# Up projection in three products: all rounded-weight products of a block ahead of all remainder products

## The chip, the core and the metric

The kernel runs on one core of one Trainium2 chip. The metric is the device time of one execution in microseconds (us), less is better. The engines are named as in the profile: PE is TensorE's matmul stream and PEld its weight loads, DVE is VectorE, ACT is ScalarE, POOL is GpSimd, SP is SyncE, whose queue issues the DMAs here.

## What is computed

The reference is a decoder trunk of two layers on 256 tokens of width 1024. Each layer has an attention part and then a feed-forward part, which is where the change lies:

```python
h = _rms_norm(x, g_pre_mlp[l])
y = jnp.square(jax.nn.relu(h @ w_up[l])) @ w_down[l]     # w_up 1024 x 4096, w_down 4096 x 1024
x = x + _rms_norm(y, g_post_mlp[l])
```

All of it is float32.

## The kernel before

**Three products for one.** Most large matmuls are done in the type fp32r on operands split in two: `hi`, the operand rounded to fp32r by ACT (a Copy), and `lo`, what the rounding left over, made by DVE (raw minus hi). A product a x w is taken as a_hi w_hi + a_hi w_lo + a_lo w_hi, all three summed in one PSUM bank. For the weights these tiles are `whi` and `wlo`, made from `wraw`, into which a DMA on SP's queue loads 512 KB (`Weights.load` and `Weights.get`, lines 418 to 446). There are 4 raw slots and 7 slots each of `whi` and `wlo` (lines 43, 421, 440, 441).

**The up projection** (`up`, lines 1319 to 1344). The 4096 columns of w_up are worked off in 8 chunks of 512. Chunk 0 has a form of its own (`up0`). Chunks 1 to 7 call `up(fc)`, and each has four blocks b of 128 columns: 2 layers x 7 chunks x 4 = 56 blocks. A block multiplies 128 columns of weights (the stationary operand, loaded into the array by an LDWEIGHTS for each matmul) with the normalized activations, transposed, in `xT`. `xT[0]` is their rounded half, `xT[1]` the remainder, and `xT[2]` is both side by side: 2 x 256 columns. For each of the 8 slices k of 128 rows there are two matmuls into one PSUM bank `ps` (tag `s`, three of them) of 512 columns:

- the wide one (line 1326): `hi[:, k]` against `xT[2][:, k]`, 512 columns. It puts w_hi x_hi into the left half of the bank and w_hi x_lo into the right half;
- the narrow one (line 1328): `lo[:, k]` against `xT[0][:, k]`, 256 columns, which adds w_lo x_hi into the right half, `ps[:, S:]`.

Behind the block, ACT copies the right half to `h` and DVE adds the left half to it (lines 1335, 1336). Behind every second block ACT and DVE make relu, square and the split of the result into `aT` (lines 1337 to 1343), the operand of the down projection. In the profile, the wide product is `s<-xT,whi`, the narrow one `s<-xT,wlo`.

**The loop around it** (lines 1385 to 1425). `up(fc + 1)` is recorded ahead of the down projection of chunk fc, so that the results of a chunk are needed only one chunk later. The down projection has, for each of 4 slices k, 2 token tiles and 2 column halves, three wide products (512 columns, `mm3`, line 598) into the banks `x` and `acc`: 12 for a k, 48 for a chunk. `then` (line 1330) is the late half of `up0`: four transposes of `h2` and their split.

**What sets the order.** Nothing runs in the order of the source by itself. `Recorder.add` (line 189) notes each operation with its dependences, and `Recorder.order` (line 243) plays a model of the engines: whenever an engine is free, it takes among the operations whose inputs are ready the one with the lowest key (the key is the place in the recording, or that of an earlier mark for loads and splits, lines 429 and 439), urgent ones first. `emit` (line 343) then issues all instructions from one line, 350, in that order. So every row of the profile bears L350, and groups are told apart by tiles.

**A narrow run elsewhere.** In the input projection, `in_chunk_T` (line 1005) has 128 columns of weights as stationary operand against 256 columns of `xT` with `mm3`, three matmuls in a row into the same half of a bank `acc`: `acc<-xT,whi` and `acc<-xT,wlo` in the profile.

Of the kernel before, what the change touches and what calls it, by code (L numbers as in the profile page):

```python
# [460 lines left out]
def trunk(nc, A, consts_in, out, sbp, pp):  # L461
    def tile(shape, dtype, name, tag=None, bufs=1):
        return nc.tile(sbp[(tag or name) not in OPERANDS], shape, dtype, name, tag, bufs)

    def psum(tag):
        return nc.tile(pp, [P, 512], F32, tag, tag, {"acc": 2, "x": 2, "s": 3, "o": 1}[tag], psum=True)

    def small(shape, name, bufs=2):
        return tile(shape, F32, name=name, tag=name, bufs=bufs)
# [49 lines left out]
    def weight(*key):  # L519
        return W.get(index[key])  # L520
# [209 lines left out]
    for l in range(DEPTH):  # L730
# [588 lines left out]
        def up(fc, then=None):  # L1319
            a = [tile([P, 4, S], F32R, name="aT", tag=f"act{j}", bufs=2) for j in range(2)]  # L1320
            for b in range(4):
                hi, lo = weight(l, "up", fc, b)

                ps = psum("s")
                for k in range(8):
                    nc.tensor.matmul(ps, hi[:, k, :], xT[2][:, k].rearrange("p j n -> p (j n)"), start=k == 0, stop=False,
                                     skip_group_check=True)
                    nc.tensor.matmul(ps[:, S:], lo[:, k, :], xT[0][:, k, :], start=False, stop=k == 7,
                                     skip_group_check=True)
                if then is not None and b == 1:  # L1330
                    then()
                if b % 2 == 0:
                    h = tokt("h")
                d = h[:, (b % 2) * S:(b % 2) * S + S]
                nc.scalar.activation(d, ps[:, S:], AF.Copy)
                nc.vector.tensor_add(d, ps[:, :S], d)
                if b % 2:
                    rl = small([P, 512], "rl")
                    nc.scalar.activation(rl, h, AF.Relu)
                    nc.vector.tensor_mul(h, rl, rl)  # L1340
                    d = [y[:, b - 1:b + 1, :].rearrange("p b n -> p (b n)") for y in a]
                    nc.scalar.activation(d[0], rl, AF.Square)
                    nc.vector.tensor_sub(d[1], h, d[0].bitcast(F32))
            return a
# [42 lines left out]
        for fc in range(8):  # L1387
            if fc < 7:
                nxt = up(fc + 1, then)
                then = None  # L1390
# [75 lines left out]
```

## Time and profile before

| | |
|---|---|
| device time, median of 3 runs | 635.33 us (635.32 to 635.46) |
| device time of the profiled execution | 635.77 us |
| its span | 634.0 us |
| mean granted clock of TensorE | 0.998 |
| busy in the span: PE, PEld, DVE, ACT | 625.5, 520.4, 480.9, 373.8 us |
| moved by DMA | 115.75 MB, 183 GB/s over the span |

The span goes from the first to the last recorded instruction; the device time has 1.77 us more around it. In the rows of a group stand: line, engine, operation, output tile <- input tiles, partitions x elements and type, count, then busy us, the mean of one in ns, and the idle time of the engine ahead of them with what ended it. A timeline row has start and duration in us first; "x2" says that two were merged, and the duration is then that of both. Matmuls overlap, and their ends are modelled, so the distance between two starts is what one costs. A row of the chain in order of time has start, duration and the engine with its output tile; "x64" says that it merges 64 instructions. A row of the waits has the us in total, how many times, and the longest. Some matmul records are missing from a trace, so counts from the program go ahead of counts of rows.

### The profile page before, as it was taken

Reading aid. Unit: us, or ns where it says so; the run is one execution under the profiler, and the core shown is the slowest. Engines: PE = TensorE matmul, PEld = TensorE weight load, DVE = VectorE, ACT = ScalarE, POOL = GpSimd, SP = SyncE. Lnnn points to the kernel's source line nnn. Section 1 sums busy time; section 2 is a strip of 40 time slices with the busy share of each in tenths; the row PEclk is TensorE's granted clock in tenths of the full one; section 3 lists DMA queues with packets and bytes.
Section 4 is the critical chain, followed back from the end, with each engine's and each line's share of the span. In section 5 each row is a group of like instructions: output and inputs, shape, how many; then the busy total and the mean of one; then the engine's idle time right before and its main releaser. Section 6 shows DMA issues by size and latency. Waiting matters only on the chain.

```text
span 634.0 us, 9913 instructions
## 1 busy us (share of the span) xinstructions
PE 625.5 (99%) x3570; PEld 520.4 (82%) x3570; DVE 480.9 (76%) x1084; ACT 373.8 (59%) x737; POOL 0.2 (0%) x4
## 2 busy tenths in 40 slices
PE   9999999999999999999999999999999999999995
PEld 6888977688888888888888988777888888888884
DVE  6899998869985665566598999987998665666544
ACT  7865676564864455456467656864658464455432
POOL 0000000000000000000000000000000000000000
PEclk9999999999999999999999999999999999999999
DMA  8998436225786666656329954432267766655601
GB/s 307 345 321 284 131 100 168 85 67 174 247 280 196 196 178 197 194 185 183 121 81 308 331 167 130 166 101 67 66 230 259 228 184 197 197 184 186 197 1 66
DMA packets 47005, 115.75 MB, mean 183 GB/s; under 512 B 4003, under 2 KB 14573, under 8 KB 46957
## 3 DMA queue, kind: packets, MB, share of 16 engines
q1 hardware_dynamic: 46956, 115.13, 56.8%
q8 instruction: 28, 0.46, 0.3%
q14 instruction: 21, 0.16, 0.1%
HBM read 114.07 MB, written 1.05 MB: 182 GB/s over the span
## 4 chain that ended last, share of the span: by engine, by line
PE 98%; DMA 1%; DVE 0%; ACT 0%; SPq 0%; issue 0%; DVEq 0%
PE s L350 35%; PE acc L350 31%; PE x L350 25%; PE o L350 7%; DMA wraw<-in_w_in_dram 1%; SPq L350 0%; DVE x L350 0%; DVE m L350 0%; DVEq L1462 0%; ACT whi L350 0%; ACT xT L350 0%; DVE rsqrt L350 0%; ACT rl L350 0%; DVEq L350 0%
## 5 line engine op out<-in xcount | busy, mean ns | idle before, releaser
L350 DVE TENSOR_TENSOR wlo<-wraw,whi 128x1024 fp32r<-128x1024 f32 (+2 forms) x196 | 230.2, 1180 | 101.8 <-ACT whi L350 100.1
L350 ACT ACTIVATE whi<-wraw 128x1024 fp32r<-128x1024 f32 (+2 forms) x196 | 199.7, 1025 | 157.0 <-PE acc L350 74.2
L350 PE MATMUL s<-xT,whi 128*128 128x512 f32 x448 | 158.5, 397 | 0.0
L350 PE MATMUL s<-xT,wlo 128*128 128x256 f32 x448 | 125.7, 281 | 0.0
L350 PEld LDWEIGHTS s<-xT,whi 128*128 128x128 f32 x448 | 84.1, 188 | 20.5
L350 PE MATMUL acc<-whi,aT 128*128 128x512 f32 x256 | 88.9, 391 | 0.0
L350 PE MATMUL x<-whi,aT 128*128 128x512 f32 x256 | 88.8, 391 | 0.0
L350 PEld LDWEIGHTS s<-xT,wlo 128*128 128x128 f32 x448 | 84.6, 189 | 0.6
L350 PEld LDWEIGHTS x<-whi,aT 128*128 128x128 f32 x256 | 47.9, 188 | 10.2
L350 PEld LDWEIGHTS acc<-whi,aT 128*128 128x128 f32 x256 | 48.0, 188 | 10.0
L350 ACT ACTIVATE pr<-pr,st 128x128 f32<-128x128 f32 (+1 forms) x96 | 42.8, 447 | 17.5 <-DVE st L350 17.1
L350 PE MATMUL acc<-wlo,aT 128*128 128x512 f32 x128 | 49.9, 390 | 0.0
L350 PE MATMUL x<-wlo,aT 128*128 128x512 f32 x128 | 49.9, 390 | 0.0
L350 PE MATMUL acc<-xT,whi 128*128 128x256 f32 x256 | 49.4, 285 | 0.0
L350 PEld LDWEIGHTS acc<-xT,whi 128*128 128x128 f32 x256 | 40.4, 190 | 2.3 <-issue 1.4
L350 PE MATMUL x<-whi,xT 128*128 128x512 f32 x112 | 37.9, 408 | 0.5 <-ACT whi L350 0.3
L350 PE MATMUL acc<-whi,xT 128*128 128x512 f32 (+1 forms) x128 | 38.2, 359 | 0.0
L350 PE MATMUL acc<-xT,wlo 128*128 128x256 f32 x128 | 36.3, 286 | 0.0
L350 ACT ACTIVATE rl<-x 128x512 f32<-128x512 f32 x24 | 14.7, 612 | 24.9 <-PE x L350 16.8
L350 PEld LDWEIGHTS acc<-wlo,aT 128*128 128x128 f32 x128 | 24.0, 188 | 5.1
L350 PEld LDWEIGHTS x<-wlo,aT 128*128 128x128 f32 x128 | 24.0, 188 | 4.6
L350 ACT ACTIVATE h<-s 128x256 f32<-128x256 f32 x56 | 20.6, 368 | 10.7 <-PE s L350 10.7
(219 smaller groups left out, 963.2 us busy)
## 6 DMA issues: line engine op xcount, KB each, us to landing
wraw<-in_w_up_dram SPq DMA_DIRECT2D x64, 512.0 KB, 3.7
wraw<-in_w_down_dram SPq DMA_DIRECT2D x64, 512.0 KB, 3.9
wraw<-in_w_in_dram SPq DMA_DIRECT2D x39, 512.0 KB, 5.0
wraw<-in_w_out_dram SPq DMA_DIRECT2D x16, 512.0 KB, 3.6
w<-in_cmp_w_k_dram SPq DMA_DIRECT2D x8, 512.0 KB, 5.4
w<-in_cmp_w_v_dram SPq DMA_DIRECT2D x8, 512.0 KB, 8.2
wraw<-in_w_in_dram SPq DMA_DIRECT2D x8, 288.0 KB, 5.1
x<-in_x_dram SPq DMA_DIRECT2D x4, 256.0 KB, 7.4
```

The source lines that it names most:

```text
L350: getattr(getattr(self.nc, op.engine), name)(*[real(v) for v in args], **{k: real(v) for k, v in kw.items()})
```

## The change

In `up`, the loop over k is cut in two. In each block the eight wide products of `hi` are recorded first, then the eight narrow ones of `lo`, where before they alternated. The first product still starts the sum in the bank (`start=k == 0`), and the last narrow one still ends it (`stop=k == 7`). No instruction is added or taken away.

```diff
@@ -1325,6 +1325,7 @@
                 for k in range(8):
                     nc.tensor.matmul(ps, hi[:, k, :], xT[2][:, k].rearrange("p j n -> p (j n)"), start=k == 0, stop=False,
                                      skip_group_check=True)
+                for k in range(8):
                     nc.tensor.matmul(ps[:, S:], lo[:, k, :], xT[0][:, k, :], start=False, stop=k == 7,
                                      skip_group_check=True)
                 if then is not None and b == 1:
```

## The prediction

> **What bounds the kernel now.** I read the page's busy line first, then its chain that ended last, to see which engine sets the end.
>
> ```profile
> span 634.0 us, 9913 instructions
> ## 1 busy us (share of the span) xinstructions
> PE 625.5 (99%) x3570; PEld 520.4 (82%) x3570; DVE 480.9 (76%) x1084; ACT 373.8 (59%) x737; POOL 0.2 (0%) x4
> ...
> PE 98%; DMA 1%; DVE 0%; ACT 0%; SPq 0%; issue 0%; DVEq 0%
> ```
>
> TensorE is busy for 99% of the span and is 98% of the chain. A busy TensorE can still hide waits, so the third view is the waits of PE alone:
>
> ```profile
> PE o L350 <- DVE warm L350: 1.2, 1, 1.2
> PE x L350 <- ACT whi L350: 0.3, 1, 0.3
> PE x L350 <- ACT xT L350: 0.2, 1, 0.2
> ```
>
> These 1.7 us are all it shows, and none is in the up projection. So what counts is the distance between the starts of successive matmuls ("pitch"), and the change can act only on that, or by making a new wait. The fourth view is the groups, for the instructions that the change moves.
>
> ```profile
> L350 PE MATMUL s<-xT,whi 128*128 128x512 f32 x448 | 158.5, 397 | 0.0
> L350 PE MATMUL s<-xT,wlo 128*128 128x256 f32 x448 | 125.7, 281 | 0.0
> ...
> L350 PEld LDWEIGHTS s<-xT,whi 128*128 128x128 f32 x448 | 84.1, 188 | 20.5
> ...
> L350 PEld LDWEIGHTS s<-xT,wlo 128*128 128x128 f32 x448 | 84.6, 189 | 0.6
> ```
>
> 448 wide products (512 columns, rounded weights) and 448 narrow ones (256 columns, remainders): 56 blocks of 8 pairs. Their means, 397 and 281 ns, overlap with the next matmul, so they are no prices. Prices come from the fifth view, the chain in order of time, where a piece is so many matmuls in so many us:
>
> ```profile
> 464.32 8.09 PE s L350 x47
> ...
> 482.88 11.29 PE s L350 x64
> 494.17 1.40 PE x L350 x6
> 495.57 1.38 PE acc L350 x6
> 496.95 1.36 PE x L350 x6
> 498.31 1.36 PE acc L350 x6
> ```
>
> The reader is to see three things. Four blocks of the up projection (64 matmuls) take 11.29 us, so 2.822 us a block and 352.8 ns a pair. The down projection behind them, all wide, runs its later passes at 1.36 / 6 = 226.7 ns, but its first twelve at 1.40 + 1.38. And the first chunk of each layer, same instructions, is quicker: 47 matmuls (24 narrow, 23 wide) in 8.09 us; 23 wide ones at 226.7 take 5.21, which leaves 2.88 / 24 = 120 ns for a narrow one, or 346.7 a pair. So there are two paces, 6 ns a pair apart, and I do not know what switches them. The timeline of PE gives the twelve more exactly:
>
> ```profile
> 494.00 0.40 PE L350 MATMUL x<-whi,aT 128*128 128x512 f32 x1
> ...
> 496.79 0.39 PE L350 MATMUL x<-whi,aT 128*128 128x512 f32 x1
> ```
>
> 2.79 / 12 = 232.5 ns for a wide product at the slow pace.
>
> **What a narrow product costs in a run.** The up projection never runs two narrow ones in a row. The input projection does (256 columns, 128x128 weights from the same kind of tile, every matmul with its own weight load, three in a row into the same half bank):
>
> ```profile
> 66.10 0.39 PE L350 MATMUL acc<-xT,whi 128*128 128x256 f32 x2
> ...
> 68.83 0.29 PE L350 MATMUL acc<-xT,wlo 128*128 128x256 f32 x1
> ```
>
> 23 matmuls start from the first to the last of these: 2.73 / 23 = 118.7 ns. With the 120 above, the narrow product has the bounds 118.7 and 120; I take 118.7, as it is the row with narrow neighbours.
>
> **The change, part by part.**
>
> *Removed and added:* nothing. 8 wide and 8 narrow products, with their 16 loads, stay in each block. Only the order of the 16 changes. The planner takes the ready instruction that was recorded first, and both orders are recorded in the loop, so the new order reaches the chip.
>
> *The pitch in the 50 slow blocks* (48 of the later chunks, and the first block of each layer): before, 2.822 us. After, 8 x 232.5 + 8 x 118.7 = 2.810 us, when a run of eight wide products keeps the pace that wide products show right behind the up projection today. That is -0.012 us a block, -0.6 us in all. With 120 ns for the narrow ones it is 2.820 us, and -0.1 us in all. With 226.7 ns for the wide ones it is 2.763 us, -0.059 a block. I take 232.5: the only place where wide products follow narrow ones now is the head of the down projection, and there the slow pace lasts for twelve of them, more than the eight of a run.
>
> *The 6 fast blocks* (three in each layer) take 8.09 + 0.23 us for three, 2.77 each. If they come to the same 2.81, they lose 0.04 each: +0.2 us.
>
> *The wait for the remainders.* In the second block of each layer PE had to go to other work, as the remainder was not there:
>
> ```profile
> 152.25 0.40 PE L350 MATMUL s<-xT,whi 128*128 128x512 f32 x1
> 152.49 0.60 PE L350 MATMUL s<-cst,h 128*128 128x128 f32 x4
> 152.85 0.71 PE L350 MATMUL x<-whi,aT 128*128 128x512 f32 x2
> 153.40 0.28 PE L350 MATMUL s<-xT,wlo 128*128 128x256 f32 x1
> ```
>
> Two wide products take 0.55 us here against 0.45 at 226.7: 0.10 us is lost. After, eight wide products stand between the first use of the rounded weights and that of the remainders, 1.86 us. -0.1 us in each of two layers, -0.2 us. What is late next is nothing that I can see: the transposes of h then wait for the end of their block instead of filling this hole.
>
> *Buffers and the other engines.* The last reader of the rounded weights is now the eighth instruction of a block, not the fifteenth; that of the remainders stays the last. ACT and DVE around one block's end:
>
> ```profile
> 507.84 1.06 ACT L350 ACTIVATE whi<-wraw 128x1024 fp32r<-128x1024 f32 x1 [1.63 <-PE s L350]
> 508.81 0.37 ACT L350 ACTIVATE h<-s 128x256 f32<-128x256 f32 x1
> ...
> 508.93 1.23 DVE L350 TENSOR_TENSOR wlo<-wraw,whi 128x1024 fp32r<-128x1024 f32 x1 [1.47 <-ACT whi L350]
> 510.07 0.42 DVE L350 TENSOR_TENSOR h<-s,h 128x256 f32<-128x256 f32 x1
> ```
>
> ACT's rounding waits for PE to free a slot. It will start about 7 x 118.7 = 0.8 us earlier, DVE's remainder follows ACT and then waits for the last narrow product itself, and the load on SP's queue that reuses the raw slot goes out up to 0.8 us earlier. Queued behind ACT's wait is only the evacuation h, which needs the block's end anyway. No DMA is added, none passes another. All this has seven weight slots and three PSUM banks of slack and is hidden by the PE stream: price 0. If that cover were gone, a block could lose the 1.23 us of one remainder; the waits of PE show no such case even now, with everything 0.8 us later. The evacuation reads both halves of the bank and still comes behind the sixteenth product.
>
> **Sum:** -0.6 + 0.2 - 0.2 = -0.6 us. The profiled execution took 635.77 us, 1.77 beside its span of 634.0; the median of the runs shown, 635.33, is 0.44 lower, and I apply the difference to it: 634.7 us.
>
> **A rule that speaks against it.** The loads: 188 ns each by the groups above, longer than a narrow pitch. Today each load that has only a narrow product as cover stands next to one that has a wide product. In a run of eight, seven loads follow each other with narrow cover only. The Trainium skill, "TensorE: Matmul & The Clock Gate", section "LDWEIGHTS (loading the stationary operand)", gives columns / 1.2 GHz, an estimate of 107 ns for 128 columns, and its section "Back-to-back issue gap" says that the spacing in a real stream is set by both the load and the matmul. By that page 256 columns stream in an estimated 109 ns, so that a run of narrow products would be left with 2 ns of slack a load, and the order of the products would be free only while nothing delays a load. The trace agrees in part: the narrow run goes at 118.7 ns with a load for each.
>
> **The rivals.**
>
> 1. *Faster: the alternation itself holds the slow pace.* If the change of width at each step causes the 6 ns, the runs go at 226.7 + 118.7: 50 x -0.059 = -3.0 us; the head of the down projection loses its excess too, 1.40 + 1.38 - 2 x 1.36 = 0.06 us in each of 12 chunks, -0.7; with the -0.2 of the wait, 631.4 us. For it: the later passes of the down projection, uniform, are fast. Against it: alternating blocks are fast too in the first chunk (8.09 us), and the twelve uniform products are slow. A mixture, in which a run loses the excess midway, gives about 633.
>
> 2. *Slower: weight loads bound the narrow runs.* Place: products 10 to 16 of each block. Price: other narrow stretches are worse than the one above, such as
>
> ```profile
> 62.79 0.36 PE L350 MATMUL acc<-xT,wlo 128*128 128x256 f32 x1
> ...
> 65.63 0.63 PE L350 MATMUL x<-kx,qS 128*128 128x512 f32 x2
> ```
>
> 23 matmuls in 2.84 us, 123.5 ns. That is 4.8 ns more on 448 products, +2.2 us on the forecast: 636.9 us. It decides (0.2% = 1.3 us above before; 0.2% is about what a measurement of this kernel can tell from no change) from 4.2 ns a narrow product above 118.7, (1.3 + 0.6) / 448. The far bound, loads not hidden at all at 188 ns, would be +31 us. Against it: this stretch holds its excess in its first start after transposes; behind that it keeps 120 ns.
>
> 3. *The change does nothing on the chip:* the planner could give back the alternation, where remainders are ready. Its keys follow the recording, so I give this no chance of its own; it would be 635.3.
>
> **How the numbers follow.** Forecast (order nearly neutral, 634.4 to 635.6): 0.42. Rival 1 with its mixture: 0.34. Rival 2, with any other reshuffling by the planner that makes PE wait: 0.24. The range reaches half into each rival: 632.0 to 637.0 us. Faster by over 0.2%: 0.34; within: 0.42; slower: 0.24.
>
> **What would show it.** In the chain, four blocks should be one piece of 64 matmuls in 11.24 us (11.05 by rival 1, 11.4 or more by rival 2). In the timeline, eight wide starts 232 ns apart and eight narrow ones 119 apart; rival 2 shows in the narrow ones alone. The first twelve of the down projection should keep their 2.78 us, and rival 1 takes them to 2.72. The hole at 152.85 should be gone, and PE's waits should be no more than the three lines above. ACT's rounding should start in mid-block. What would make me wrong: the two paces, whose cause I do not know; a pace that spreads from the runs into the 36 later products of each down chunk would cost more than all terms here.

## The result and the profile after

The changed kernel takes 633.49 us (median of 7 runs, 633.02 to 633.63), the kernel before 635.46 us beside it (7 runs, 635.02 to 635.94). The ratio is 0.9967, 95% interval 0.9955 to 0.9979: 0.33% faster, 2.0 us. That is inside the range, but not the case forecast as likeliest (nearly neutral, 634.7 us); it lies where rival 1 put its mixture, at about 633. The forecast gain was 0.6 us, less than a third of the one measured.

First the page of the changed kernel, the lines that answer to those shown of before:

```profile
span 631.8 us, 9913 instructions
PE 622.8 (99%) x3570; PEld 520.6 (82%) x3570; DVE 482.1 (76%) x1084; ACT 373.6 (59%) x737; POOL 0.2 (0%) x4
...
PE 96%; DMA 2%; DVE 1%; ACT 1%; issue 0%; SPq 0%; DVEq 0%
```

As many instructions as before, the same engine at the end, a span that is 2.2 us shorter. The waits of PE are the same three as before:

```profile
PE o L350 <- DVE warm L350: 1.2, 1, 1.2
PE x L350 <- ACT whi L350: 0.7, 1, 0.7
PE x L350 <- ACT xT L350: 0.2, 1, 0.2
```

The middle one is longer (0.7 us, 0.3 before), but it falls at 7.7 us, long ahead of the first up projection, and in a second profile of the changed kernel (e_after, below) it is 1.4: it is no part of the change. Now its chain in order of time (start, duration, engine and output tile, instructions merged):

```profile
459.26 11.59 PE s L350 x68
...
481.75 11.15 PE s L350 x64
492.90 1.39 PE x L350 x6
494.28 1.36 PE acc L350 x6
```

Four blocks went from 11.29 to 11.15 us; this piece stands in 12 chunks, so -1.7 us. The head of the down projection behind them, its first twelve products, went from 1.40 + 1.38 to 1.39 + 1.36: -0.03 us, -0.4 in the 12. The first chunk of a layer is one piece of 68 now (64 products and the four transposes), 11.59 us. The chain of the kernel before has it in three pieces, of which the last is the 8.09 us of the prediction:

```profile
460.36 3.49 PE s L350 x21
463.85 0.47 PE x L350 x2
```

That is 12.05 us together, with two down products in it, which cost 0.45 elsewhere. So nothing was won there. -1.7 and -0.4 give -2.1 us: the measured 2.0 lies in the up projection and the twelve products behind it.

Where inside the 11.15? The timeline of PE. In a merged row the duration ends with the last instruction, so the distance to the next row's start is what a run costs:

```profile
481.59 1.98 PE L350 MATMUL s<-xT,whi 128*128 128x512 f32 x8
483.40 1.11 PE L350 MATMUL s<-xT,wlo 128*128 128x256 f32 x8
484.35 2.00 PE L350 MATMUL s<-xT,whi 128*128 128x512 f32 x8
486.19 1.12 PE L350 MATMUL s<-xT,wlo 128*128 128x256 f32 x8
487.15 2.00 PE L350 MATMUL s<-xT,whi 128*128 128x512 f32 x8
```

The first wide run of a chunk, behind the down projection's wide products, takes 483.40 - 481.59 = 1.81 us, 226 ns each. The later ones, behind a narrow run, take 1.84 (230 ns each). The narrow runs take 0.95 to 0.96, 119 ns each. So a wide run behind a narrow one is 0.03 us longer than its pure price, and so is the head of the down projection. If each product at the slow pace costs 232.5 - 226.7 = 5.8 ns too much, 30 ns are five of them, not eight and not twelve. The trace, which holds the starts to the nanosecond, shows these five: from 484.35 us on, the eight distances are 234, 235, 229, 232, 231, then 227, 226, 227 ns.

### The profile page after: what moved, and what is told of

Its sections match the earlier page's. It is cut to its first block, busy times and chain, and to the rows that moved or that the text cites. A ratio compares the mean times of both kernels' runs of the same rounds, so it can differ in the third digit from the quotient of the medians.

```text
span 631.8 us, 9913 instructions
## 1 busy us (share of the span) xinstructions
PE 622.8 (99%) x3570; PEld 520.6 (82%) x3570; DVE 482.1 (76%) x1084; ACT 373.6 (59%) x737; POOL 0.2 (0%) x4
## 4 chain that ended last, share of the span: by engine, by line
PE 96%; DMA 2%; DVE 1%; ACT 1%; issue 0%; SPq 0%; DVEq 0%
PE s L350 35%; PE acc L350 30%; PE x L350 24%; PE o L350 7%; DMA wraw<-in_w_in_dram 1%; DMA xt<-in_xT_dram 1%; DVE q L350 0%; ACT whi L350 0%; ACT xT L350 0%; ACT q_tok L350 0%; DVE rope L350 0%; SPq L350 0%; DVE x L350 0%; DVE m L350 0%; DVEq L1463 0%
## 5 line engine op out<-in xcount | busy, mean ns | idle before, releaser
L350 PE MATMUL s<-xT,whi 128*128 128x512 f32 x448 | 112.0, 392 | 0.0
L350 PEld LDWEIGHTS s<-xT,whi 128*128 128x128 f32 x448 | 81.4, 189 | 15.2
L350 PEld LDWEIGHTS s<-xT,wlo 128*128 128x128 f32 x448 | 61.1, 190 | 4.4
L350 PE MATMUL s<-xT,wlo 128*128 128x256 f32 x448 | 62.5, 282 | 0.0
```

The source lines that it names most:

```text
L350: getattr(getattr(self.nc, op.engine), name)(*[real(v) for v in args], **{k: real(v) for k, v in kw.items()})
```

## The experiments

The question is what makes wide products slow. Three theories. *Changes:* each step from narrow to wide costs something, so what counts is how many such steps a chunk has. *Counts:* each narrow product leaves a debt that the wide ones behind it pay, so the order is nearly free. *Release:* the gain comes from the weight slots that come free earlier, not from PE. The pure price of four blocks is 32 x 226.7 + 32 x 119.4 = 11.07 us. The diffs below are shortened, and words in brackets stand for code. Those of e_fours, e_late, e_wide and e_quad are written against the changed kernel, the others against the kernel before; only e_fours, e_late and e_wide show removed lines. All times stand beside the kernel before on the same chip: 635.73 us in the first and the last group, 635.51 and 635.54 in the others.

### Two blocks at a time (e_pairs)

```diff
+                if b % 2 == 0:
+                    two = []
+                    for i in range(2):
+                        two.append((*weight(l, "up", fc, b + i), psum("s")))
+                    for hi, lo, ps in two:
+                        for k in range(8):
+                            (wide product)
+                    for hi, lo, ps in two:
+                        for k in range(8):
+                            (narrow product)
+                ps = two[b % 2][2]
```

> Two blocks at a time: 16 wide products, then 16 narrow ones. Without any slow pace four blocks would take 11.07 us (32 x 226.7 + 32 x 119.4 ns). The changed kernel shows 11.15, that is 28 ns for each of its three changes from narrow to wide inside a chunk, and 2.75 instead of 2.72 us for the first twelve products of the down projection. Theory of changes (a fixed 28 ns for each change from narrow to wide): one change inside a chunk instead of three, 11.10 us, head of the down projection 2.75; 14 chunks x 0.056 = 0.8 us less than the changed kernel, 632.7 us. Theory of counts (3.5 ns for each narrow product, repaid by the wide ones behind it): 56 ns behind each run of 16, 11.13 us, head 2.78, no gain, 633.5 us. Theory of release (the gain comes from the weight slot that comes free earlier): the slots come free later than in the changed kernel, so 633.5 us or slower.

Measured: 633.0 us, ratio 0.9957 (0.9943 to 0.9971). The chain of e_pairs:

```profile
481.44 11.11 PE s L350 x64
492.54 1.39 PE x L350 x6
493.93 1.36 PE acc L350 x6
```

11.11 us against 11.10 by changes and 11.13 by counts, and the head is 2.75, as behind a run of eight. Sixteen narrow products leave no more behind than eight do. The theory of counts falls on the head (it asked for 2.78). The gain over the changed kernel is read from the chain, 0.04 us in each of 12 chunks; the times alone do not tell the two apart (0.9957 here, 0.9967 there, with overlapping intervals). On release this run says little: the remainders of the first block come free later, but the rounded weights of the second come free earlier, behind the sixteenth of 32 products where the changed kernel has them behind the 24th.

### Groups of four (e_fours)

```diff
-                for k in range(8):
+                for k in range(4):
                     (wide product)
-                for k in range(8):
+                for k in range(4):
                     (narrow product)
+                for k in range(4, 8): (wide), then for k in range(4, 8): (narrow)
```

> Groups of four: 4 wide, 4 narrow, 4 wide, 4 narrow in each block. Theory of changes: seven changes inside a chunk, each paid by at most four wide products at 5.8 ns, 23 ns: 11.07 + 0.16 = 11.23 us for four blocks, +1.1 us on the changed kernel, 634.6 us. Theory of counts: 14 ns a run, 11.17 us, head of the down projection 2.73 to 2.74, 633.7 us. Theory of release: the last wide product is the twelfth of the block instead of the eighth, half the gain lost, 634.5 us with no change of pitch in the runs.

Measured: 634.76 us, ratio 0.9981 (0.9972 to 0.999). The timeline of e_fours:

```profile
482.40 1.07 PE L350 MATMUL s<-xT,whi 128*128 128x512 f32 x4
483.31 0.64 PE L350 MATMUL s<-xT,wlo 128*128 128x256 f32 x4
483.78 1.09 PE L350 MATMUL s<-xT,whi 128*128 128x512 f32 x4
484.71 0.63 PE L350 MATMUL s<-xT,wlo 128*128 128x256 f32 x4
```

The first four wide products take 0.91 us (227 ns each), the next four, behind narrow ones, 0.93 (232.5): all four are slow. The narrow ones take 0.47 (117.5), a little less than in longer runs. The chain of e_fours:

```profile
482.56 11.20 PE s L350 x64
493.76 1.40 PE x L350 x6
495.15 1.37 PE acc L350 x6
```

11.20 us lie between the 11.23 by changes and the 11.17 by counts; the time, 634.76, is that of changes (634.6). The head is 2.77, longer than behind runs of eight, where counts asked for 2.73 to 2.74.

### Grouped, but released late (e_late)

```diff
-                for k in range(8): (wide)
-                for k in range(8): (narrow)
+                for k in range(7): (wide)
+                for k in range(7): (narrow)
+                for k in range(7, 8): (wide), then (narrow)
```

> 7 wide, 7 narrow, 1 wide, 1 narrow in each block: grouped, but the rounded weights come free as late as before the change. Theory of release: back to the time before the change, 635.4 us. Theory of changes: a lone wide product pays 6 ns more in each block and the run behind the lone narrow one pays 28: 11.07 + 4 x 0.006 + 3 x 0.028 = 11.18 us for four blocks, 633.9 us. Theory of counts: the lone wide product repays 6 of the 24 ns that seven narrow ones left, the rest is paid behind: 11.15 us, 633.5 us.

Measured: 634.57 us, ratio 0.9978 (0.9966 to 0.9991). The chain of e_late has:

```profile
482.32 11.19 PE s L350 x64
493.51 1.40 PE x L350 x6
494.91 1.38 PE acc L350 x6
```

And its timeline:

```profile
484.58 0.40 PE L350 MATMUL s<-xT,whi 128*128 128x512 f32 x1
484.81 0.28 PE L350 MATMUL s<-xT,wlo 128*128 128x256 f32 x1
484.93 1.80 PE L350 MATMUL s<-xT,whi 128*128 128x512 f32 x7
486.57 0.98 PE L350 MATMUL s<-xT,wlo 128*128 128x256 f32 x7
```

Release had asked for the whole gain to go (635.4). About half stays, and the half that went is on PE: behind the lone narrow product, seven wide ones take 1.64 us, 234 ns each on average (six of the seven starts are 231 to 241 ns apart, one 224). (11.29 - 11.19) x 12 = 1.2 us, which is what was measured. So release is out. Nor had PE a wait in the up projection, before the change or here, that an earlier release could have shortened. The surprise is that seven wide products are not enough to repay here, while five are behind a pure narrow run: the twelve products of the down projection's head are slow again, too, as in the kernel before.

### No narrow products (e_wide)

```diff
-                    nc.tensor.matmul(ps[:, S:], lo[:, k, :], xT[0][:, k, :], start=False, stop=k == 7,
+                    nc.tensor.matmul(ps, lo[:, k, :], xT[2][:, k].rearrange("p j n -> p (j n)"), start=False, stop=k == 7,
```

This adds the product of the two remainders, which the kernel before leaves out.

> The remainders, too, are multiplied with both halves of the activations, 512 columns: no narrow product is left (the product of the two remainders is added, which the reference's float32 holds too). If narrow products are what makes the wide ones slow: every start 226.7 ns behind the last, 64 in 14.51 us, head of the down projection 2.72 us, device time 633.5 + 14 x 3.36 = 680.5 us. If the slow pace belongs to the up projection's own operands, whatever the widths: 64 x 232.5 = 14.88 us, head 2.78, about 686 us.

Measured: 680.13 us. The chain of e_wide:

```profile
508.18 14.51 PE s L350 x64
522.68 1.36 PE x L350 x6
524.04 1.36 PE acc L350 x6
```

14.51 / 64 = 226.7 ns, and the head of the down projection has no excess. So the slow pace does not belong to the up projection's operands; it comes only with the narrow products beside the wide ones. (The width, 256 columns, and the half bank that they write go together here; no run takes them apart.)

### Four blocks at a time (e_quad), beside the changed kernel (e_after)

```diff
+                if b == 0:
+                    four = []
+                    for i in range(4):
+                        hi, lo = weight(l, "up", fc, i)
+                        ps = psum("s" if i < 3 else "o")
+                        four.append((lo, ps))
+                        for k in range(8): (wide product)
+                lo, ps = four[b]
                 for k in range(8): (narrow product)
```

> All four blocks of a chunk together (the fourth in the bank o): 32 wide products, then 32 narrow ones, no change from narrow to wide inside a chunk. Theory of changes (about 30 ns each): four blocks at the pure pace, 32 x 226.7 + 32 x 119.4 = 11.07 us, head of the down projection 2.75 us as in the pairs; 14 x (11.15 - 11.07) = 1.1 us less than the changed kernel. Theory against it: narrow products in a run of 32 outrun their weight loads, so that their pitch rises above 119.4; or the four remainder tiles that are held until the end starve DVE and the loads behind it, and PE shows new waits. Either would show as more than 11.11 us, the piece of the pairs.

> The changed kernel itself, beside the group of four blocks on the same chip: 11.15 us for four blocks, 2.75 us for the head of the down projection, 1.1 us slower than the group of four if changes cost 28 ns each.

Measured: 632.69 us for the four (632.49 to 633.23; ratio 0.9955, 0.9943 to 0.9968) and 633.41 us for the changed kernel (633.23 to 633.67; 0.9964, 0.9951 to 0.9978). The chain of e_quad, one chunk:

```profile
481.05 5.44 PE s L350 x24
486.49 1.81 PE o L350 x8
488.30 2.87 PE s L350 x24
491.17 0.96 PE o L350 x8
492.13 1.39 PE x L350 x6
493.52 1.36 PE acc L350 x6
```

11.08 us, the pure price but for 0.01; 32 narrow products in a row keep 3.83 / 32 = 119.7 ns, so their loads do not bound them, and no new wait of PE came up: the waits are the same three, that on ACT 1.1 us at the kernel's start, where e_after has 1.4. The gain over the changed kernel is 0.7 us, where 1.1 was expected: 14 x 0.07 would be 1.0. This kernel and e_pairs are the quickest here; their ratios, 0.9955 and 0.9957, do not tell them apart.

### Why has one alternation two paces? (e_ins, e_gap)

Before the change, the first chunk of each layer alternated at 346.7 ns a pair, behind a wait. Two kernels, both made from the kernel before, ask whether the wait or the neighbours did it.

```diff
 e_ins, behind each wide product:
+                    if b == 1 and k == 0:
+                        po = psum("o")
+                        for j in range(4):
+                            nc.tensor.transpose(po[:, j * P:j * P + P], ident, ident)
+                        for j in range(2):
+                            nc.tensor.matmul(po, hi[:, j, :], xT[2][:, j]..., start=True, stop=True)
 e_gap, ahead of the products:
+                if b == 1:
+                    z = small([P, P], "zero")
+                    nc.vector.tensor_sub(z, d[:, :P], d[:, :P])
+                    nc.vector.tensor_add(lo[:, 0, :], lo[:, 0, :].bitcast(F32), z)
```

> The alternating kernel, with four transposes of a constant and two wide products into an unused bank put between the first wide and the first narrow product of block 1 of each chunk (their results are not used): the same sequence on PE as in the first chunk of the kernel before, but with nothing to wait for. If that sequence set the quick pace of the first chunk (346.7 ns a pair), the 24 pairs behind it run at 346.7 in every chunk. If the wait did, they stay at 352.8 here, and the chunk is longer by the inserted work alone, about 0.8 us.

> The alternating kernel, with the first remainder slice of block 1 in each chunk rewritten by DVE (zero added) once block 0 is evacuated, so that the products of block 1 wait for it and block 2 and one product of the down projection go ahead. If a wait of PE switches the alternation to the quick pace, the pairs behind that product run at 346.7 ns in every chunk; if the pace depends only on what stands next to what, at 352.8.

Measured in a single execution of each: 646.24 us for e_ins and 635.47 us for e_gap. Two chunks of the chain of e_ins:

```profile
492.81 8.25 PE s L350 x47
...
515.91 8.09 PE s L350 x47
```

The same 47 products behind the same insertion, at the slow pace in one chunk (8.25 us) and at the quick one in the next (8.09). In this kernel 10 of the 12 later chunks are quick behind the insertion, without any wait; the second chunk of each layer is slow. The widths are the same in both; only the starts differ by a few ns: from each of the two inserted wide products to the next start it is 318 and 231 ns in a slow chunk, 315 and 235 in a quick one. In e_gap, the pairs are quick in all chunks but one from the point where block 2's first wide product stands next to one of block 1's, ahead of the wait. In that one chunk the pairs turn quick, too, and go back to the slow pace behind two starts that come 0.2 us late. So a wait is not what is needed, and a fixed price for each change falls as well: the alternation has two paces for one and the same order of widths.

### One neighbouring pair of wide products (e_hh, e_shift, e_hh1, e_back)

In these the narrow product of slice i follows the wide product of slice i + 1 instead of i, over a part of the chunk, so that the only new thing on PE is one place with two wide neighbours, and one with two narrow ones at the end (in e_shift, one of each for every block). `wide(i)` and `narrow(i)` are the two products of slice i % 8 in block i // 8.

```diff
 e_hh: the lag starts behind the eighth pair
+                for i in range(8 * b, 8 * b + 8):
+                    if i <= 8:
+                        wide(i)
+                    if i >= 8 and i < 31:
+                        wide(i + 1)
+                    narrow(i)
 e_hh1: behind the first pair
+                    if i <= 1: wide(i)
+                    if i >= 1 and i < 31: wide(i + 1)
 e_back: in block 1 alone
+                    if i <= 8 or i >= 16: wide(i)
+                    if i >= 8 and i < 15: wide(i + 1)
 e_shift: in each block: wide, (wide, narrow) seven times, narrow
```

> The alternating kernel with one change: from block 1 of each chunk on, the narrow products lag by one wide product, so that one pair of neighbouring wide products stands behind the eighth pair, the alternation goes on behind it, and the chunk ends on two narrow ones. Nothing waits. Theory of order (two neighbouring wide products amid an alternation set it to the quick pace, as in the kernel with the gap): 8 pairs at 352.8 ns, then 23 at 346.7, 11.14 us for four blocks, 633.4 us, as good as the changed kernel without its grouping. Theory of waiting (in the kernel with the gap, and in the first chunk of the kernel before, a wait of PE made the pace quick): all pairs at 352.8 ns, 11.29 us, 635.5 us. By the theory of changes with a fixed price for each change the alternation can have only one pace, 11.28 us.

> The narrow products lag by one in every block: wide, wide, narrow, wide, narrow ... wide, narrow, narrow. Theory of order: the two neighbouring wide products at the head of blocks 1, 2 and 3 set the quick pace, block 0 (behind the down projection's wide products) is slow: 11.14 us for four blocks or less, 633.4 us. Theory of waiting: slow pace throughout, about 11.28 us, 635.3 us.

> The narrow products lag by one from the second wide product of each chunk on: wide, narrow, wide, wide, narrow, wide, narrow ... narrow, narrow. Theory of order (one pair of neighbouring wide products behind a narrow one sets the quick pace, which then lasts): 30 pairs at 346.7 ns, 11.10 us for four blocks, 632.9 us, as good as the group of four blocks. If the alternation must have run for some pairs first (the lag came behind eight pairs before), 352.8 ns and 11.28 us, 635.4 us.

> The narrow products lag by one in block 1 alone: eight pairs, wide, seven pairs, narrow, sixteen pairs. If two neighbouring narrow products undo what two neighbouring wide ones do, the seven pairs run at 346.7 ns and the last sixteen at 352.8: 11.29 - 7 x 0.006 = 11.25 us for four blocks, 634.9 us. If the quick pace lasts whatever follows, 11.15 us and 633.6 us.

Measured: e_hh 633.59 us, ratio 0.9968 (0.9955 to 0.998). e_shift 635.04, 0.9989 (0.998 to 0.9998). e_hh1 635.12, 0.9989 (0.998 to 0.9998). e_back 633.39, 0.9959 (0.9947 to 0.9972). Four blocks in the chains of e_hh, e_shift, e_hh1 and e_back, in this order:

```profile
481.89 11.15 PE s L350 x64
```

```profile
482.17 11.26 PE s L350 x64
```

```profile
482.26 11.28 PE s L350 x64
```

```profile
481.25 11.15 PE s L350 x64
```

The timeline of e_hh around the one place where it differs from the kernel before:

```profile
484.19 0.40 PE L350 MATMUL s<-xT,whi 128*128 128x512 f32 x1
484.42 0.28 PE L350 MATMUL s<-xT,wlo 128*128 128x256 f32 x1
484.54 0.64 PE L350 MATMUL s<-xT,whi 128*128 128x512 f32 x2
485.02 0.28 PE L350 MATMUL s<-xT,wlo 128*128 128x256 f32 x1
485.14 0.39 PE L350 MATMUL s<-xT,whi 128*128 128x512 f32 x1
485.37 0.28 PE L350 MATMUL s<-xT,wlo 128*128 128x256 f32 x1
```

The row "x2" is the pair of wide neighbours. Before it, the eight pairs take 2.81 us, 351 ns each with the first wide product still at 226; behind it, 346.7 (from the narrow product at 485.02 to that at 492.30 there are 21 pairs, 7.28 us). In the order of widths, one narrow product has moved to the end of the chunk. That gives the whole gain of the change, without grouping anything. The theory of order forecast this, but falls on the next kernel: the same neighbours behind the first pair of a chunk do next to nothing, e_hh1 stays at 352.5 (11.28 / 32). The quick pace then outlasts two narrow neighbours: e_back runs its sixteen last pairs at 346.7, where going back to 352.8 was expected. And in e_shift, where the two narrow and the two wide neighbours come together at each block's border, the pace is between, 351.9 (11.26 / 32).

So the slow pace is a state of the stream that an alternation can stay in or out of for as long as it goes on. What the state is, these runs do not tell: it is not a wait that the profile shows, and not the widths of the nearest neighbours. That stays open.

Its form can be read from the starts, though. At the slow pace the distances repeat after three pairs: in the kernel before, from 483.05 us on, wide 232, narrow 118, wide 241, narrow 120, wide 236, narrow 113 ns, 1060 ns in all. At the quick pace every pair is alike, 230 for the wide and 116 or 117 for the narrow; behind the two narrow neighbours of e_back two pairs take turns, 231 + 112 and 232 + 118 ns. So the narrow product costs 117 ns on average at either pace, and the 6 ns are in the wide ones. And the second wide neighbour follows the longest step of the cycle (240 to 242 ns) in e_hh and e_back, where the pace changes, but the step of 234 ns in e_hh1, where it does not. Whether this place in the cycle decides is not shown: no run varies it alone.

## Why the prediction was right or wrong, step by step

- *PE's pitch bounds the kernel, and the change acts only there:* right. The instructions stayed, PE still has no wait in the up projection, and the pieces of the chain add up to 2.1 us where 2.0 were measured.
- *The pitch in the 50 slow blocks, -0.6 us:* the failed step. That a block costs the sum of its two runs was right; that a wide run keeps the slow pace to its end was not, and 8 x 232.5 was too much. The run behind the down projection goes at 226 ns (1.81 us for eight), the others at 230 (1.84), since only about five products of a run are slow, not all eight. I had taken the twelve products at the head of the down projection as the measure (start by start, ten of them are off the pace, 224 to 241 ns, and the last two at 227), but these followed an alternation; behind a run of narrow products, the head itself has only half that excess (0.03 us for 0.06). The block measures 11.15 / 4 = 2.788, not 2.810: -0.035 on the 48 blocks of the later chunks, -1.7 us.
- *The narrow product at 118.7 ns:* right; 119 in runs of eight, 119.4 in sixteen, 119.7 in 32, as a run begins with 113 and 119 ns and then keeps 120. The other bound, 120 from the first chunk, was split wrongly, though its sum holds: that alternation has 230 ns for a wide and 117 for a narrow product, not 226.7 and 120.
- *The head of the down projection keeps its 2.78 us:* wrong, 2.75, another -0.4 us.
- *The 6 fast blocks +0.2, the wait for the remainders -0.2:* their sum came true, 11.59 us against 11.60 without the two down products, but by luck, as neither part did. The fast blocks did not come to 2.81 but to 2.79 (1.84 + 0.95), +0.02 each. And the 0.55 us of the two down products was not time lost in a wait: behind the same four transposes, with nothing to wait for, the two inserted products of e_ins take 0.55 as well, and the first two wide products of the changed kernel 314 + 231 ns.
- *Buffers and other engines at no cost:* right, and e_late shows that the release is no part of the gain. ACT's rounding does come into mid-block where a slot is what it waits for: at 489.19 us PE releases it, 0.75 us ahead of the block's end at 489.94. Elsewhere it meets the next limit, its input, a DMA. Of the changed kernel:

```profile
486.89 1.06 ACT L350 ACTIVATE whi<-wraw 128x1024 fp32r<-128x1024 f32 x1 [0.74 <-DMA wraw<-in_w_up_dram]
489.19 1.06 ACT L350 ACTIVATE whi<-wraw 128x1024 fp32r<-128x1024 f32 x1 [0.96 <-PE s L350]
```

- *Rival 1, the alternation holds the slow pace:* it came half true, as the mixture. Its full form, no slow product at all (11.05 us for four blocks), needed 32 products in a row (11.08). As worded, that the change of width at each step causes the 6 ns, it falls: e_hh and e_back change the width almost as often and are quick.
- *Rival 2, loads bound the narrow runs:* out. Runs of up to 32 keep 119.7 ns, against the 123 that it needed. So the reading that I took from the Trainium skill, "TensorE: Matmul & The Clock Gate", sections "LDWEIGHTS (loading the stationary operand)" and "Back-to-back issue gap", an estimated 2 ns of slack for a load beside a narrow product, did not turn into a loss here.
- *The two paces, "whose cause I do not know":* named as what could make me wrong, and it did.

## What to carry to other kernels

When TensorE is 99% busy, read the distances of the starts, not the busy share: 6 ns in each pair of a regular stream were 2 us here, with no wait to be seen. If the trace shows the same instructions at two paces, the stream's order is worth a trial before any explanation: products of one width in long runs were the best form here (11.08 us with runs of 32 against 11.29 alternating). A price that was read behind one kind of stream, as the twelve slow products were, holds behind that kind of stream only.

## What I had not expected of the hardware

One order of matmuls, 512 and 256 columns by turns, runs at 352.8 or at 346.7 ns a pair, and keeps its pace over at least 21 pairs; one more wide product behind the eighth pair switches it, behind the first it does not. The slow form is a cycle of three pairs (1060 ns), in which the wide products cost 232, 241 and 236 ns by turns. After it the wide products are slow, too, ten of them at 233 ns on average before they are back at 226.7, though they have no narrow neighbour any more. The granted clock was 0.996 to 0.999 in all these runs, and does not go with the pace.
